# Differential attention in an encoder block: combining a tile's two score maps on GpSimd, undivided by the first map's sum, instead of on VectorE

## The chip, the cores and the metric

The kernel runs on one core of a Trainium2 chip, as one launch. The metric is device time in microseconds (us): median of three runs for the kernel before. The engines are TensorE (PE; its weight loads are listed as PEld), VectorE (DVE), ScalarE (ACT), GpSimd (POOL) and SyncE (SP), which issues the DMAs. Each works through its own list of instructions in order, and they wait for each other by semaphores.

## The reference

One encoder block for 1024 tokens of width 1024, with 16 meta tokens put in front (1040 keys), all in float32: an RMS norm, a projection, two attention branches, a gated merge, an output projection, then a SwiGLU feed-forward part and a last norm. The edit concerns branch A, differential attention with 4 heads, each with two score maps and one set of values of width 128:

```python
s1 = einsum('bqhd,bkhd->bhqk', q1, k1) * scale + bias
s2 = einsum('bqhd,bkhd->bhqk', q2, k2) * scale + bias
attn = softmax(s1, axis=-1) - lam * softmax(s2, axis=-1)
y = einsum('bhqk,bkhe->bqhe', attn, v)
...
y = rms_norm(y, subln_g) * (1.0 - lambda_init)   # y * rsqrt(mean(y*y) + EPS) * gain
```

Branch B is attention in a window; both branches are merged through sigmoid gates, which are projections of the block's input.

## The kernel before

The program is built by one long function, and a scheduler orders the instructions of ACT, DVE, POOL and SP by a simulated timeline. In branch A's attention PE is excepted: its order is the order in which the code issues its instructions, so it is written out by hand there.

**Stages.** First the input is normed and projected and branch B's attention is done (0 to some 330 us). Then follows branch A's attention, together with the projections of the gates (about 330 to 620 us). Then come the branches' output products, the merge, the output projection, and the feed-forward part by a scheme of seven products.

**Branch A's attention.** The work goes over 4 heads (h) and 8 tiles (t) of 128 queries, 32 tiles; "tile 3.2" is tile 2 of head 3. A string of slots, `SLOTS = "sgsgsngsgsgstntnt"` (in the last head `"sgsgsngsgsstntnt"`), says what PE is given for one tile after the other: `s` a step of this tile's scores, `g` a step of a gate projection (three matmuls of 512 columns, L199, which fill PE while other engines work), `t` a step of the transposes of the tile before (T_LAG = 1), `n` a step of the values or the norm of a pair of tiles before. All six `s` stand ahead of the first `t`. At the start of a head ten more gate steps stand in between, thirty at the first.

For one tile `scores_a` does the second map first (m = 1), then the first (m = 0). For each, PE makes the scores in three chunks of 352, 352 and 336 keys (L588, into banks of PSUM that rotate five deep under the tag "sc"; the transposes and the norm use the same banks). DVE subtracts the distance bias while it moves them to SBUF and keeps the running minimum (L594; the last chunk in two pieces, `no_dist` and `dist`). ACT takes the exponential of the 128x1040 map in place and sums its rows into `dn` (L599, followed by a read of the accumulator). DVE inverts the sum (L600). For m = 1 POOL scales the map by 1/sum and by -lambda (L602). For m = 0 DVE then makes the combined map, first map times 1/sum plus scaled second map (L605, one pass over 128x1040), and POOL copies 32 columns for the meta tokens (L606). The first map lies in one of two tiles `s0s`, the second in `s1` with two buffers.

One tile later `transpose_a` transposes the combined map on PE in groups of 4, 4 and 1 (L617, tile `apt`), ACT and DVE copy the result out as a high and a low part (L620, L621). `values_a` multiplies it with the values (L630) for pairs of tiles. `normed_a`, once for four tiles, squares the values (L637), sums the squares on PE (L643), forms mean plus EPS on DVE (L645), raises it to -1/2 on POOL (L646), and applies it (L651, L652).

Beside this, each of 16 gate columns needs its weights split into two parts: a copy on ACT (L111, `wh_c`) and a 128x1024 subtraction on POOL (L112, `wl_c`), and ACT copies the gate's results out (L539).

Of the kernel before, what the change touches and what calls it, by code (L numbers as in the profile page):

```python
# [9 lines left out]
F32 = mybir.dt.float32  # L10
F32R = mybir.dt.float32r
I32 = mybir.dt.int32
AF = mybir.ActivationFunctionType
ALU = mybir.AluOpType
# [4 lines left out]
P = 128  # L19
# [3 lines left out]
L = S + NM  # L23
# [8 lines left out]
EPS = 1e-6  # L32
# [2 lines left out]
SC = 5  # L35
N_WAIT = 3
PP2 = 2
COMBINE_POOL = (0, 1, 2, 3)
SLOTS = "sgsgsngsgsgstntnt"
SLOTS_LAST = "sgsgsngsgsstntnt"  # L40
S_BUFS = (2, 2)
# [28 lines left out]
def encoder_block(ctx: ExitStack, tc: tile.TileContext, x, meta, norm_mix, w_in, lq1, lk1, lq2, lk2,  # L70
                  subln, sink, w_ba, w_bb, w_o, norm_ffn, w_g, w_u, w_d, norm_final, out, dbg=None):
    nc = tc.nc
# [8 lines left out]
    def pool(name, side="left", space=None, bufs=1):  # L81
        kw = {} if space is None else {"space": space}
        if space is not DRAM:
            kw["reuse_waits"] = "tile"
        cm = tc.tile_pool(name=name, bufs=bufs, side=side, **kw)
        p = cm.__enter__()
        return p, lambda: cm.__exit__(None, None, None)
# [5 lines left out]
    def bank(p, tag, name, bufs):  # L93
        return p.tile([P, 512], F32, tag=tag, name=name, bufs=bufs)
# [267 lines left out]
    xts, xns, done, early = {}, {}, [], []  # L362
# [102 lines left out]
    neglam = acon.tile([P, 1], F32, name="neglam")  # L465
# [84 lines left out]
    apool, close_apool = pool("apool")  # L550
# [21 lines left out]
        nc.sync.dma_start(f32(v)[2 * NM:3 * NM, 0, 8, :], va_d[h][:NM, 1, 8, :])  # L572
        return qs, ks, v

    def scores_a(h, t, ld, s):
        slope = 2.0 ** -(2 * (h + 1))
        qs, ks, _ = ld
        nm = f"{h}_{t}"
        mn = small.tile([P, 2, 4], F32, tag="amn", name=f"amn_{nm}")
        dn = small.tile([P, 2], F32, tag="adn", name=f"adn_{nm}")  # L580
        u0 = 896 - t * P
        for m in (1, 0):
            s[m] = s0s[t % 2] if m == 0 else apool.tile([P, L], F32, tag="s1", name=f"as1_{nm}", bufs=S_BUFS[1])
            low = far_a
            for i, (k0, n) in enumerate(A_CHUNKS):
                ps = bank(psum2, "sc", f"aps_{nm}_{m}_{k0}", SC)
                for vv in range(2):
                    nc.tensor.matmul(ps[:, :n], qs[m][:, t * P:(t + 1) * P], ks[m][:, vv, k0:k0 + n],  # L588
                                     start=(vv == 0), stop=(vv == 1))
                parts = [(k0, min(k0 + n, S), dist[:, u0 + k0:u0 + min(k0 + n, S)])]  # L590
                if k0 + n > S:
                    parts.insert(0, (S, L, no_dist))
                for j, (a, b, far_by) in enumerate(parts):
                    nc.vector.tensor_tensor_reduce(s[m][:, a:b], ps[:, a - k0:b - k0], far_by, slope, low,  # L594
                                                   ALU.add, ALU.min, mn[:, m, i + j:i + j + 1])
                    low = mn[:, m, i + j:i + j + 1]
                if i < 2:
                    yield
            nc.scalar.activation(s[m][:, 0:L], s[m][:, 0:L], AF.Exp, bias=low, scale=-1.0, accum_out=dn[:, m:m + 1])  # L599
            nc.vector.reciprocal(dn[:, m:m + 1], dn[:, m:m + 1])  # L600
            if m:
                (nc.gpsimd if t % 4 in COMBINE_POOL else nc.vector).tensor_scalar(  # L602
                    s[1][:, 0:L], s[1][:, 0:L], dn[:, 1:2], neglam, ALU.mult, ALU.mult)
            yield
        nc.vector.scalar_tensor_tensor(s[0][:, 0:L], s[0][:, 0:L], dn[:, 0:1], s[1][:, 0:L], ALU.mult, ALU.add)  # L605
        nc.gpsimd.tensor_copy(s[0][:, L:L + 2 * NM].rearrange("p (a k) -> p a k", a=2),  # L606
                              s[0][:, S:L].unsqueeze(1).broadcast_to([P, 2, NM]))

    def transpose_a(h, t, s, at_):
        i = t % 2  # L610
        for b in range(3):
            nb = 4 if b < 2 else 1
            kp = P
            pt = bank(psum2, "sc", f"apt_{h}_{t}_{b}", SC).rearrange("p (k t) -> p k t", k=4)
            for j in range(nb):
                k = 4 * b + j
                nc.tensor.transpose(pt[:kp, j, :], s[:, k * P:k * P + kp], ident)  # L617
            hi = at_[:kp, 4 * b:4 * b + nb, 0, i * P:(i + 1) * P]
            lo = at_[:, 4 * b:4 * b + nb, 1, i * P:(i + 1) * P] if b < 2 else hi[:NM]
            nc.scalar.activation(hi, pt[:kp, :nb], AF.Copy)  # L620
            nc.vector.tensor_tensor(lo, pt[:lo.shape[0], :nb], f32(hi)[:lo.shape[0]], ALU.subtract)  # L621
            yield

    def values_a(h, t, v, at_, py):
        cols = slice(t % 4 // 2 * 256, t % 4 // 2 * 256 + 256)
        for part in range(3):
            for k in range(3 * part, 3 * part + 3):
                kp = P
                for j, (a, b) in enumerate(((0, 0), (0, 1), (1, 0)) if k < 8 else ((0, 0),)):
                    nc.tensor.matmul(py[:, cols], v[:kp, a, k, :], at_[:kp, k, b, :],  # L630
                                     start=(k == 0 and j == 0), stop=(k == 8))
            yield

    def normed_a(h, c, py):
        nm = f"{h}_{c}"
        ysq = apool.tile([P, 512], F32, tag="ysq", name=f"ysq_{nm}", bufs=1)
        nc.scalar.activation(ysq, py, AF.Square)  # L637
        yg = apool.tile([P, 512], F32, tag="yg", name=f"yg_{nm}", bufs=2)
        nc.scalar.activation(yg, py, AF.Copy, scale=gsub)
        yield  # L640
        pst = bank(psum2, "sc", f"apst_{nm}", SC)
        for i in range(4):
            nc.tensor.matmul(pst[:, i:i + 1], ysq[:, i * P:(i + 1) * P], ones, start=True, stop=True)  # L643
        f = small.tile([P, 4], F32, tag="af", name=f"af_{nm}", bufs=2)
        nc.vector.tensor_scalar(f, pst[:, 0:4], 1.0 / P, EPS, ALU.mult, ALU.add)  # L645
        nc.gpsimd.tensor_tensor(f, f, neg_half, ALU.pow)  # L646
        for _ in range(N_WAIT):
            yield
        pf = bank(psum2, "sc", f"apf_{nm}", SC)
        for i in range(4):  # L650
            nc.tensor.transpose(pf[:, i * P:(i + 1) * P], f[:, i:i + 1].broadcast_to([P, P]), ident)  # L651
        nc.vector.tensor_tensor(yg, yg, pf, ALU.mult)  # L652
        nc.sync.dma_start(ya_d[h][:, c * 512:c * 512 + 512], yg)
        yield
# [5 lines left out]
    def fill(n):  # L660
        while n > 0 and n_gates[0] > 0:
            n, n_gates[0] = n - 1, n_gates[0] - 1
            next(gates, None)


    acc = [None]

    def turn(done):
        h, t, s, at_, v = done
        yield from transpose_a(h, t, s[0], at_)  # L670

    def later(done):
        h, t, s, at_, v = done
        if t % 4 == 1:
            acc[0] = bank(psum2, "acc", f"apy_{h}_{t}", 1)
        yield from values_a(h, t, v, at_, acc[0])
        if t % 4 == 3:
            yield from normed_a(h, t // 4, acc[0])

    order_pe = tc.manual_schedule(engines={mybir.EngineType.PE})  # L680
    order_pe.__enter__()
    tiles, turning, tail = [], iter(()), []

    def step_tail():
        while tail and next(tail[0], True):
            tail.pop(0)

    for n in range(AH * NT + T_LAG):
        scoring, turning = iter(()), iter(())
        if n < AH * NT:  # L690
            h, t = divmod(n, NT)
            if t == 0:
                ld = load_a(h)
                fill(G_HEAD if h else G_FIRST)
            if t % 2 == 0:
                at_ = apool.tile([P, 9, 2, 256], F32R, tag="at", name=f"at{h}_{t}", bufs=AT_BUFS)
            s = [None, None]
            tiles.append((h, t, s, at_, ld[2]))
            scoring = scores_a(h, t, ld, s)
        if n >= T_LAG:  # L700
            turning = turn(tiles[n - T_LAG])
        for what in SLOTS if n < 3 * NT else SLOTS_LAST:
            if what == "s":
                next(scoring, None)
            elif what == "t":
                next(turning, None)
            elif what == "n":
                step_tail()
            else:
                fill(1)  # L710
        for _ in scoring:
            pass
        for _ in turning:
            pass
        if n >= T_LAG and tiles[n - T_LAG][1] % 2:
            tail.append(later(tiles[n - T_LAG]))
# [488 lines left out]
    for n in range(nf, len(steps)):  # L1205
# [4 lines left out]
        if p in LOADS:  # L1210
            at, half, col = LOADS[p]
            if at <= j < at + 4:
                t, cols = 4 * half + j - at, slice(col * 512, col * 512 + 512)
# [60 lines left out]
```

## Time and profile before

| | |
|---|---|
| device time, median of 3 runs | 1466.98 us (1464.96 to 1467.93) |
| the profiled execution | 1467.45 us |
| its span, first to last instruction | 1465.7 us (1.75 us lie around it) |
| mean granted clock of TensorE | 0.997 |
| busy in the span | PE 98%, DVE 59%, ACT 45%, POOL 36% |

A row of a table by stretch gives a stretch of the span, its length, then busy time of each engine (number of instructions), the granted clock of PE, the share of DMA. A row of groups gives line, engine, operation, output and inputs, shape, count, then busy us and mean ns, then idle us of the engine just ahead of it with what ended it. A timeline row gives start and duration in us, engine, line, operation, output<-inputs, and in brackets the idle time ahead of it and who ended it. A busy PE is not PE at its peak, since matmuls overlap. Names are cut: `as` is either map, `adn` its sums, `amn` the minima.

### The profile page before, as it was taken

The numbers are of one execution on the slowest core, as the hardware profiler recorded it, in microseconds if no ns is written. First come the engines' busy times: TensorE is split into PE (matmuls) and PEld (weight loads), VectorE is DVE, ScalarE is ACT, GpSimd is POOL, SyncE is SP. The second block draws the span as 40 slices with busy tenths as digits, with TensorE's granted clock in tenths as the row PEclk, the third lists the DMA queues.
The fourth block names the chain that finished last, engine by engine and source line by source line (L and its number), as shares of the span: only waits on it lengthen the run. The fifth ranks groups of instructions, "written<-read, shape, count | busy, mean of one in ns | idle before, by whom it ended". The sixth has DMA issues, their size and how long they took to land.

```text
span 1465.7 us, 21002 instructions
## 1 busy us (share of the span) xinstructions
PE 1439.6 (98%) x7353; PEld 1237.5 (84%) x7353; DVE 859.0 (59%) x1664; ACT 654.6 (45%) x1237; POOL 529.8 (36%) x502
## 2 busy tenths in 40 slices
PE   6999999999999999999999999999999999999998
PEld 6988989988898989877888878888888888888886
DVE  6356426528686868423613876555555554787667
ACT  5365436525455555445412744333333333444454
POOL 4143223313323232223822566454545442000444
PEclk9999999999999999999999999999999999999999
DMA  7334353272524251086531434333333323954443
GB/s 233 89 98 115 111 127 98 77 204 96 152 73 145 73 153 66 31 277 196 169 126 61 141 122 135 126 103 98 108 103 105 101 93 102 345 201 141 125 124 142
DMA packets 155577, 189.96 MB, mean 130 GB/s; under 512 B 16128, under 2 KB 101568, under 8 KB 155472
## 3 DMA queue, kind: packets, MB, share of 16 engines
q1 hardware_dynamic: 155472, 188.63, 40.9%
q8 instruction: 58, 0.95, 0.3%
q14 instruction: 47, 0.39, 0.1%
HBM read 128.09 MB, written 53.94 MB: 124 GB/s over the span
## 4 chain that ended last, share of the span: by engine, by line
PE 86%; POOL 4%; issue 4%; DMA 3%; ACT 1%; DVE 1%; SPq 1%; POOLq 0%; ACTq 0%; DVEq 0%
PE pg L1055 26%; PE pp_g L199 10%; PE pd L1149 8%; PE ppa L532 6%; PE po L832 6%; PE aps L588 4%; PE apy L630 3%; PE pp_va L199 3%; PE pp_qb L199 3%; PE pp_qa L199 3%; PE pp_ka L199 3%; POOL oa L112 3%; PE apt L617 2%; PE bpt L337 2%; PE bpy L343 2%
## 5 line engine op out<-in xcount | busy, mean ns | idle before, releaser
L1055 PE MATMUL pg<-t,wop 128*128 128x512 f32 x1056 | 242.9, 389 | 0.2 <-POOL wop L112 0.2
L1055 PEld LDWEIGHTS pg<-t,wop 128*128 128x128 f32 x1056 | 198.1, 188 | 41.7 <-POOL wop L112 0.6
L112 POOL TENSOR_TENSOR wop<-wf,wop 128x512 fp32r<-128x512 f32 x128 | 171.6, 1345 | 165.9 <-ACT wop L111 152.1
L1149 PE MATMUL pd<-ob,oa 128*128 128x512 f32 x924 | 210.2, 389 | 0.8 <-POOL oa L112 0.4
L1149 PEld LDWEIGHTS pd<-ob,oa 128*128 128x128 f32 x924 | 173.3, 188 | 37.6 <-POOL oa L112 0.8
L1055 PE MATMUL pg<-b,wop 128*128 128x512 f32 x792 | 184.0, 390 | 2.7 <-DVE c L1064 2.7
L1055 PEld LDWEIGHTS pg<-b,wop 128*128 128x128 f32 x792 | 148.3, 188 | 34.2 <-issue 2.4
L112 POOL TENSOR_TENSOR wl_c<-w_c,wh_c 128x1024 fp32r<-128x1024 f32 x31 | 74.9, 2418 | 155.2 <-ACT wh_c L111 144.8
L111 ACT ACTIVATE wop<-wf 128x512 fp32r<-128x512 f32 x128 | 80.2, 631 | 85.2 <-PE pg L1055 48.4
L599 ACT ACTIVATE as<-as,amn 128x1040 f32<-128x1040 f32 x64 | 74.5, 1165 | 72.7 <-DVE amn L594 72.7
L112 POOL TENSOR_TENSOR oa<-ra,oa 128x512 fp32r<-128x512 f32 x33 | 44.0, 1335 | 170.8 <-ACT oa L111 169.4
L199 PE MATMUL pp_g<-hT_hi,wh_c 128*128 128x512 f32 x256 | 101.4, 396 | 0.6 <-DMA g_d<-gate_stage 0.6
L199 PE MATMUL pp_g<-hT_hi,wl_c 128*128 128x512 f32 x256 | 100.9, 394 | 0.0
L199 PE MATMUL pp_g<-hT_lo,wh_c 128*128 128x512 f32 x256 | 100.9, 394 | 0.0
L111 ACT ACTIVATE oa<-ra 128x512 fp32r<-128x512 f32 x77 | 48.7, 632 | 107.7 <-PE pd L1149 50.2
L588 PE MATMUL aps<-ak,aq 128*128 128x352 f32 (+1 forms) x384 | 92.6, 326 | 0.0
L832 PE MATMUL po<-woh,mT 128*128 128x512 f32 x384 | 88.0, 390 | 0.0
L890 DVE TENSOR_TENSOR s<-wf,wf 128x512 f32<-128x512 f32 x22 | 26.8, 1217 | 103.9 <-DMA wf<-in_w_ff_gate_dram 56.2
L832 PEld LDWEIGHTS po<-woh,mT 128*128 128x128 f32 x384 | 71.9, 188 | 14.8
L588 PEld LDWEIGHTS aps<-ak,aq 128*128 128x128 f32 x384 | 69.6, 188 | 14.0
L594 DVE CUSTOM_DVE_ANT_0 as<-aps,dist,amn 128x352 f32<-128x352 f32 (+1 forms) x128 | 71.3, 564 | 10.4 <-PE aps L588 8.4
L324 POOL TENSOR_SCALAR bs<-bs,bdn 128x432 f32<-128x432 f32 (+1 forms) x64 | 37.0, 596 | 94.8 <-DVE bdn L322 81.4
(249 smaller groups left out, 2943.1 us busy)
## 6 DMA issues: line engine op xcount, KB each, us to landing
ra<-aop SPq DMA_DIRECT2D x77, 256.0 KB, 2.6
w_c<-in_w_in_dram SPq DMA_DIRECT2D x33, 512.0 KB, 4.0
wf<-in_w_ff_gate_dram SPq DMA_DIRECT2D x24, 512.0 KB, 3.8
wf<-in_w_ff_up_dram SPq DMA_DIRECT2D x24, 512.0 KB, 3.8
aop<-as SPq DMA_DIRECT2D x44, 256.0 KB, 2.1
aop<-c SPq DMA_DIRECT2D x33, 256.0 KB, 2.0
g_d<-gate_stage SPq DMA_DIRECT2D x32, 256.0 KB, 2.0
gt<-g_d SPq DMA_DIRECT2D x32, 256.0 KB, 3.4
```

The source lines that it names most:

```text
L111: nc.scalar.activation(hi, src, AF.Copy)
L112: lo_eng.tensor_tensor(lo, src, f32(hi), ALU.subtract)
L199: nc.tensor.matmul(ps[:, :n], a[:, c, :], b[:, c, at:at + n], start=(c == 0 and i == 0), stop=(c == DC - 1 and i == 2))
L324: nc.gpsimd.tensor_scalar(st[:, r, :W], st[:, r, :W], dn[:, r:r + 1], 1.0, ALU.mult, ALU.mult)
L532: nc.tensor.matmul(ps, w[:, a, j, :], src[j][:, b, tk], start=(j == 0 and n == 0), stop=(j == 3 and n == 2))
L588: nc.tensor.matmul(ps[:, :n], qs[m][:, t * P:(t + 1) * P], ks[m][:, vv, k0:k0 + n], start=(vv == 0), stop=(vv == 1))
L594: nc.vector.tensor_tensor_reduce(s[m][:, a:b], ps[:, a - k0:b - k0], far_by, slope, low, ALU.add, ALU.min, mn[:, m, i + j:i + j + 1])
L599: nc.scalar.activation(s[m][:, 0:L], s[m][:, 0:L], AF.Exp, bias=low, scale=-1.0, accum_out=dn[:, m:m + 1])
L630: nc.tensor.matmul(py[:, cols], v[:kp, a, k, :], at_[:kp, k, b, :], start=(k == 0 and j == 0), stop=(k == 8))
L832: nc.tensor.matmul(ps, mT[:, c, a, t * P:(t + 1) * P], wos[q, c][:, b], start=(c == 0 and n == 0), stop=(c == DC - 1 and n == 2))
L1055: nc.tensor.matmul(ps, op[:, x, c, :], b[:, y, c, :], start=(p in (1, 2, 5) and c == 0 and n == 0), stop=(p in (4, 2, 3) and c == 3 and n ...
L1149: nc.tensor.matmul(ps[u], oa[:, a, u * P:(u + 1) * P], ob[:, b, :], start=(p in (1, 2, 5) and j == 0 and k == 0), stop=(p in (2, 3, 4) and ...
```

## The change

The combined map is left undivided by the first map's sum d0. With d1 the second map's sum, the map is now e0 + c*e1 with c = -lambda*d0/d1, which is d0 times the map of before. The values come out d0 times as large, and so the norm's constant EPS becomes EPS*d0*d0 for that row, which gives the same normed values. The sums d0 are kept for four tiles in a tile `dns` with three buffers, since the norm needs them later.

DVE no longer makes the 128x1040 combination, nor inverts d0. It makes c (128x1). POOL scales the second map by c, which needs both sums and so both exponentials, and then adds it to the first.

```diff
-COMBINE_POOL = (0, 1, 2, 3)
...
-    def scores_a(h, t, ld, s):
+    def scores_a(h, t, ld, s, dns):
...
+        dn0, dn1, c = dns[:, t % 4:t % 4 + 1], dn[:, 0:1], dn[:, 1:2]
...
-            nc.scalar.activation(s[m][:, 0:L], s[m][:, 0:L], AF.Exp, bias=low, scale=-1.0, accum_out=dn[:, m:m + 1])
-            nc.vector.reciprocal(dn[:, m:m + 1], dn[:, m:m + 1])
+            nc.scalar.activation(s[m][:, 0:L], s[m][:, 0:L], AF.Exp, bias=low, scale=-1.0, accum_out=dn1 if m else dn0)
             if m:
-                (nc.gpsimd if t % 4 in COMBINE_POOL else nc.vector).tensor_scalar(
-                    s[1][:, 0:L], s[1][:, 0:L], dn[:, 1:2], neglam, ALU.mult, ALU.mult)
+                nc.vector.reciprocal(dn1, dn1)
             yield
-        nc.vector.scalar_tensor_tensor(s[0][:, 0:L], s[0][:, 0:L], dn[:, 0:1], s[1][:, 0:L], ALU.mult, ALU.add)
+
+        nc.vector.tensor_scalar(c, dn0, dn1, neglam, ALU.mult, ALU.mult)
+        nc.gpsimd.tensor_scalar(s[1][:, 0:L], s[1][:, 0:L], c, 1.0, ALU.mult, ALU.mult)
+        nc.gpsimd.tensor_tensor(s[0][:, 0:L], s[0][:, 0:L], s[1][:, 0:L], ALU.add)
...
-    def normed_a(h, c, py):
+    def normed_a(h, c, py, dn0):
...
-        nc.vector.tensor_scalar(f, pst[:, 0:4], 1.0 / P, EPS, ALU.mult, ALU.add)
+        nc.vector.scalar_tensor_tensor(dn0, dn0, EPS, dn0, ALU.mult, ALU.mult)
+        nc.vector.scalar_tensor_tensor(f, pst[:, 0:4], 1.0 / P, dn0, ALU.mult, ALU.add)
```

`turn` and `later` pass the new tile on, and one is made for every fourth tile. The new kernel's lines lie one lower up to the score loop (L111 becomes L110) and one or two higher behind it (L606 becomes L607, L617 L618, L621 L622, L646 L648). Its L604 is c, L605 the scaling, L606 the addition.

The scheduler orders ACT, DVE and POOL anew in this stage; the orders of PE and SP stay as they were. On POOL, around tile 1.2, the order was as follows (`as_1_2` is the second map of tile 1.2, `as_0` and `as_1` the two tiles for first maps, `wl_c` a weight split, `af` the power of a norm, `av` the next head's values):

```order
L602 TENSOR_SCALAR as_1_1_4360<-as_1_1_4360,adn_1_4359,neglam 128x1040
L569 MEMSET av_4223 128x128
L606 COPY as_1_3424<-as_1_3424 128x32
L602 TENSOR_SCALAR as_1_2_4459<-as_1_2_4459,adn_2_4458,neglam 128x1040
L646 TENSOR_TENSOR af_1_4522<-af_1_4522,neg_half 128x4
L112 TENSOR_TENSOR wl_c_4854<-w_c_4851,wh_c_4853 128x1024
L606 COPY as_0_3423<-as_0_3423 128x32
```

Now it is:

```order
L605 TENSOR_SCALAR as_1_1_4364<-as_1_1_4364,adn_1_4363 128x1040
L568 MEMSET av_4226 128x128
L606 TENSOR_TENSOR as_1_3424<-as_1_3424,as_1_1_4364 128x1040
L607 COPY as_1_3424<-as_1_3424 128x32
L648 TENSOR_TENSOR af_1_4524<-af_1_4524,neg_half 128x4
L605 TENSOR_SCALAR as_1_2_4463<-as_1_2_4463,adn_2_4462 128x1040
L111 TENSOR_TENSOR wl_c_4859<-w_c_4856,wh_c_4858 128x1024
L606 TENSOR_TENSOR as_0_3423<-as_0_3423,as_1_2_4463 128x1040
L607 COPY as_0_3423<-as_0_3423 128x32
```

The power now stands ahead of the tile's scaling, and the weight split between its scaling and its addition.

On ACT, around tile 3.2, the order was as follows (`wh_c` is the copy that the next split needs, `as_3_2` the second map of the tile, the next L599 its first map, `apt_1` the transposes of tile 3.1):

```order
L620 ACTIVATE at_0_5842<-apt_0_2_6014 128x128
L111 ACTIVATE wh_c_6461<-w_c_6459 128x1024
L539 COPY gate_stage<-pp_g_512_5935 128x512
L599 ACTIVATE as_3_2_6023,adn_2_6022<-as_3_2_6023,amn_2_6021 128x1040
L620 ACTIVATE at_0_5842<-apt_1_0_6074 128x4x128
L599 ACTIVATE as_0_3423,adn_2_6022<-as_0_3423,amn_2_6021 128x1040
```

Now it is:

```order
L621 ACTIVATE at_0_5853<-apt_0_2_6024 128x128
L599 ACTIVATE as_3_2_6035,adn_2_6034<-as_3_2_6035,amn_2_6033 128x1040
L110 ACTIVATE wh_c_6476<-w_c_6474 128x1024
L538 COPY gate_stage<-pp_g_512_5947 128x512
L621 ACTIVATE at_0_5853<-apt_1_0_6084 128x4x128
L599 ACTIVATE as_0_3423,dns_0_5854<-as_0_3423,amn_2_6033 128x1040
```

The tile's first exponential now stands ahead of the weight copy and of the gate's copy, which stood ahead of it. The same holds for tiles 0.6, 2.2 and 3.6. In the last tiles of a group of four (0.3, 0.7, 1.3, 2.3, 2.7, 3.3 and 3.7) ACT's second exponential also moved ahead of one or more of the copies of transposes (L620).

More of the change, by code (lines that the diff above doesn't have):

```diff
@@ L668, in turn @@
     def turn(done):
-        h, t, s, at_, v = done
+        h, t, s, at_, v, _ = done
         yield from transpose_a(h, t, s[0], at_)
     def later(done):
-        h, t, s, at_, v = done
+        h, t, s, at_, v, dn0 = done
         if t % 4 == 1:
@@ L677, in later @@
         if t % 4 == 3:
-            yield from normed_a(h, t // 4, acc[0])
+            yield from normed_a(h, t // 4, acc[0], dn0)
     order_pe = tc.manual_schedule(engines={mybir.EngineType.PE})
@@ L697, in encoder_block @@
             s = [None, None]
-            tiles.append((h, t, s, at_, ld[2]))
-            scoring = scores_a(h, t, ld, s)
+            if t % 4 == 0:
+                dn0 = apool.tile([P, 4], F32, tag="dns", name=f"dns_{h}_{t}", bufs=3)
+            tiles.append((h, t, s, at_, ld[2], dn0))
+            scoring = scores_a(h, t, ld, s, dn0)
         if n >= T_LAG:
```

## The prediction

> **What bounds the kernel now.** I read the page first, its row of busy times:
>
> ```profile
> PE 1439.6 (98%) x7353; PEld 1237.5 (84%) x7353; DVE 859.0 (59%) x1664; ACT 654.6 (45%) x1237; POOL 529.8 (36%) x502
> ```
>
> TensorE (PE) works 98% of the span, so only what stops or lengthens PE changes the time. The edited instructions all lie in branch A's attention; next comes the table by stretch for it, then the waits of PE in 330 to 610 us, then the groups by line:
>
> ```profile
> 334.00:606.00 272.00, 272.00 (x1672) 246.62 (x1670) 212.73 (x708) 147.00 (x273) 82.35 (x86) 1.00 0.31 99
> PE pp_g L199 <- DMA g_d<-gate_stage: 0.6, 1, 0.6
> L605 DVE SCALAR_TENSOR_TENSOR as<-as,adn,as 128x1040 f32<-128x1040 f32 x32 | 41.5, 1297 | 1.8 <-DVE adn L600 0.5
> L602 POOL TENSOR_SCALAR as<-as,adn,neglam 128x1040 f32<-128x1040 f32 x32 | 38.9, 1214 | 75.4 <-DVE adn L600 75.4
> L646 POOL TENSOR_TENSOR af<-af,neg_half 128x4 f32<-128x4 f32 x7 | 7.2, 1027 | 4.4 <-DVE af L645 4.4
> L112 POOL TENSOR_TENSOR wl_c<-w_c,wh_c 128x1024 fp32r<-128x1024 f32 x12 | 29.4, 2449 | 39.2 <-ACT wh_c L111 39.1
> ```
>
> The first row gives busy us of PE, PEld, DVE, ACT and POOL: in 272 us PE was busy for 272, VectorE (DVE) for 213, GpSimd (POOL) for 82. PE waits 0.6 us in the stage. So the 41.5 us that DVE is relieved of (L605) are worth at most that 0.6 us by themselves. What the edit can cost is a late operand for PE: PE's order is fixed, and the transposes L617 of a tile wait for the combined map. How early that map is now, in a usual tile (head 1, tile 4), shows in the timeline (start, duration):
>
> ```profile
> 434.24 0.16 DVE L600 RECIPROCAL adn<-adn 128x1 f32<-128x1 f32 x1
> 434.50 1.21 POOL L602 TENSOR_SCALAR as<-as,adn,neglam 128x1040 f32<-128x1040 f32 x1 [3.56 <-DVE adn L600]
> 437.37 0.16 DVE L600 RECIPROCAL adn<-adn 128x1 f32<-128x1 f32 x1
> 438.04 1.29 DVE L605 SCALAR_TENSOR_TENSOR as<-as,adn,as 128x1040 f32<-128x1040 f32 x1
> 442.77 0.49 PE L617 MATMUL apt<-ident,as 128*128 128x128 f32 x3
> ```
>
> The map is ready at 439.33 and its first transpose starts at 442.77: 3.44 us in hand.
>
> **The change, priced.** Per tile DVE loses a L605 (1.30 us) and the second reciprocal (0.16), and gains one 128x1 product, taken at the reciprocal's 0.16. POOL keeps its scaling pass (1.21), but behind the second exponential now, and gains a 128x1040 addition. That addition is not in the trace. The row of equal kind, the 128x1024 subtraction of L112, shows 2.45 us on average in this stage, 2.42 undisturbed; times 1040/1024 that is 2.46, my value. Its ends: not below the one-input pass of the same size, 1.21; not above 3.01, the longest such row:
>
> ```profile
> 421.26 0.16 DVE L600 RECIPROCAL adn<-adn 128x1 f32<-128x1 f32 x1
> 421.92 1.29 DVE L605 SCALAR_TENSOR_TENSOR as<-as,adn,as 128x1040 f32<-128x1040 f32 x1
> 419.62 1.21 POOL L602 TENSOR_SCALAR as<-as,adn,neglam 128x1040 f32<-128x1040 f32 x1 [5.21 <-DVE adn L600]
> 422.47 3.01 POOL L112 TENSOR_TENSOR wl_c<-w_c,wh_c 128x1024 fp32r<-128x1024 f32 x1 [0.64 <-ACT wh_c L111]
> 425.59 0.60 PE L617 MATMUL apt<-ident,as 128*128 128x128 f32 x4
> ```
>
> That split runs 0.6 us long, and a L605 of DVE was under way for its first 0.74 us. Every L605 leaves the stage, so I keep the undisturbed 2.46; at 3.01 the sum below would grow by 5 us (0.55 in each stop, and three more tiles stop). The Trainium skill ("SBUF — State Buffer", on the port pair that VectorE and GpSimd share) says that a VectorE instruction with two SBUF inputs and a GpSimd instruction that reads SBUF keep each other waiting. By that rule, too, the addition would take its undisturbed time, as the reductions of the stage read one operand from PSUM; the long row agrees with it.
>
> The chain after the second exponential is then: product 0.16, handover to POOL 0.10 (434.40 to 434.50 above), scaling 1.21, addition 2.46, handover to PE 0.15: **4.08 us**, counted from where the second reciprocal starts now. In the usual tile 437.37 + 4.08 = 441.45, before 442.77: no stall. I took the distance from second reciprocal to first transpose for all 32 tiles from the same view; the first and the last of them:
>
> ```profile
> 338.88 0.16 DVE L600 RECIPROCAL adn<-adn 128x1 f32<-128x1 f32 x1
> 341.01 0.33 PE L617 MATMUL apt<-ident,as 128*128 128x128 f32 x1
> 602.30 0.16 DVE L600 RECIPROCAL adn<-adn 128x1 f32<-128x1 f32 x1 [0.59 <-ACT as L599]
> 604.02 0.30 PE L617 MATMUL apt<-ident,as 128*128 128x128 f32 x1
> ```
>
> Distances are 2.13 and 1.72, so the shortages are 1.95 and 2.36. Of the others 23 are long enough (4.2 to 12.6). The short ones, as head.tile with the shortage: 0.1 1.41, 0.2 0.70, 0.4 0.13, 2.6 0.17, 3.2 1.51, 3.3 0.97, 3.6 1.50. Tile 1.2 (4.33) is long enough by itself, but POOL's new order puts a weight split of 2.42 between its scaling and its addition: 2.42 − 0.25 = 2.17.
>
> Shortages of neighbours don't add. PE has issued the scores of tile t+1 before it stops for tile t, so the stop also gives tile t+1's map time: its own stop is its shortage less the one before. 0.1 falls to 0, 3.3 to 0, 3.7 to 0.86. Sum: 1.95 + 0.70 + 0.13 + 2.17 + 0.17 + 1.51 + 1.50 + 0.86 = **9.0 us**.
>
> Two corrections. In tiles 0.6, 2.2, 3.2 and 3.6 the new order of ScalarE (ACT) puts the tile's first exponential ahead of a weight copy that feeds a POOL split, and POOL has that split and the power L646 ahead of the scaling. So far, in 3.2:
>
> ```profile
> 560.20 1.06 ACT L111 ACTIVATE wh_c<-w_c 128x1024 fp32r<-128x1024 f32 x1 [2.40 <-PE pp_g L199]
> 560.51 0.55 DVE L594 CUSTOM_DVE_ANT_0 as<-aps,dist,amn 128x320 f32<-128x320 f32 x1
> 561.63 1.16 ACT L599 ACTIVATE as<-as,amn 128x1040 f32<-128x1040 f32 x1
> 561.34 2.39 POOL L112 TENSOR_TENSOR wl_c<-w_c,wh_c 128x1024 fp32r<-128x1024 f32 x1 [3.38 <-ACT wh_c L111]
> 563.69 1.03 POOL L646 TENSOR_TENSOR af<-af,neg_half 128x4 f32<-128x4 f32 x1
> 564.32 0.19 ACT L599 ACTIVATION_READ_ACCUMULATOR as<-as,amn 128x1 f32 x1
> 564.91 0.16 DVE L600 RECIPROCAL adn<-adn 128x1 f32<-128x1 f32 x1
> 567.48 0.38 PE L617 MATMUL apt<-ident,as 128*128 128x128 f32 x2
> ```
>
> The first exponential needs a reduction that ends at 561.06. Without the 1.3 us of a L605 ahead of it that becomes about 559.75; the exponential with its read lasts 1.25, so the copy starts near 561.0 instead of 560.20, 0.8 us later. Copy, split and power follow (1.06, 2.39, 1.03, with 0.04 between), and scaling can start near 565.5; the chain above had it at 564.91 + 0.26 = 565.17. That is +0.3 each for 3.2 and 3.6. In 0.6 and 2.2 I take the slip as 0.9; their distance of 4.21 has 0.13 to spare, so about +0.75 each. Together +2.1. Against it, DVE no longer has L605 ahead of what the product waits for: in 3.2 the exponential's sum is read by 564.51 and the reciprocal starts 0.40 later. I take 0.4 off each of four stops (0.2, 3.2, 3.6, 3.7): −1.6. Sum 9.0 + 2.1 − 1.6 = **9.5 us**. The profiled execution took 1467.45, 0.47 above the median: 1467.45 + 9.5 = **1477**.
>
> Costed at nothing: eight 128x4 steps for the norm's constant (DVE, 0.16 each, long before use); the 128x32 copy behind the addition (0.21), covered by two groups of four transposes that need only the addition; the weight splits that slip by 1 to 4 us. A copy starts when PE lets go of the buffer, which is when it begins the column before, and that is every 26 us here:
>
> ```profile
> 421.33 1.06 ACT L111 ACTIVATE wh_c<-w_c 128x1024 fp32r<-128x1024 f32 x1
> 447.66 1.06 ACT L111 ACTIVATE wh_c<-w_c 128x1024 fp32r<-128x1024 f32 x1 [0.57 <-PE pp_g L199]
> ```
>
> So a split has some 20 us before PE needs it. Without such cover each step costs what it lasts or slips. Loads and stores keep their order, so no DMA moves. What comes late next is the release of PSUM banks: in most last tiles of a group of four ACT and DVE now serve the second exponential and the product ahead of the copies of the tile before's transposes, whose banks PE's next scores need. In 3.3 that release comes about 1.7 us after PE would want the bank, but PE has stopped 1.5 us in 3.2 by then; so I add nothing there.
>
> **Rivals.** *A. The stops above: 1473 to 1481.* *B. Relief eats most of the stops.* If DVE's backlog hides 1.3 us in each short tile, what remains is 0.0 (no L605 runs before it) with 1.95 and 1.2, whose split is fixed, with 2.17 less 0.4: 3.7 us, 1471. *C, not slower.* Same mechanism, further. In the last tile the reduction that the exponential waits for runs late behind L605 of the tile before:
>
> ```profile
> 596.92 0.32 PE L588 MATMUL aps<-ak,aq 128*128 128x352 f32 x1
> 600.37 0.54 DVE L594 CUSTOM_DVE_ANT_0 as<-aps,dist,amn 128x320 f32<-128x320 f32 x1
> ```
>
> Scores at 596.92, reduction at 600.37. If relief brings products forward by more than each shortage, from about 2.2 us on, PE never stops: 1467. Against it: a L605 is only 1.30, and nothing precedes tile 0.0. Gain is bounded by the 0.6 us wait. *D. Stops also slow PE's clock.* These are two idle stretches of PE and the table by stretch behind the first (PE busy, granted clock, DMA):
>
> ```profile
> 684.75 0.50 PE L532 MATMUL ppa<-ya,wbha 128*128 128x512 f32 x1 [1.66 <-ACT ya L111]
> 686.00:688.00 2.00, 1.74 (x6) 0.61 0.86 271
> 688.00:690.00 2.00, 2.00 (x5) 0.54 0.85 257
> 855.46 4.81 PE L1055 MATMUL pg<-b,wop 128*128 128x512 f32 x20 [1.99 <-DVE c L1064]
> 856.00:858.00 2.00, 2.00 (x10) 1.00 0.03 8
> ```
>
> After 1.66 us idle the clock fell to half for some 3.4 us (0.39 x 2 + 0.46 x 2 = 1.7 us lost); after 1.99 us it stayed full. So a stop of 1.5 to 2.2 us can cost 1.7 more. Four or five such stops make 7 to 8 us: 1485. The Trainium skill ("TensorE: Matmul & The Clock Gate", on the gate's two states) asks for an idle window of about 3.4 us; by it D would not occur, yet the first stretch shows that half of it can do.
>
> **How the numbers follow.** A 0.58, B 0.14, C 0.09, D 0.19. A is the likeliest, so its 1477 is the forecast. With the addition at 1.21 the same sum leaves 3.0 us of stops, or 3.5 with the corrections (1471); at 3.01 it makes 14.5 (1482), and with two of D's slow stretches 1485.5. The range is 1470 to 1486: it leaves out C (0.09) and the far end of D (some 0.06). About 0.2%, 2.9 us, is what a measurement tells from no change. C is within it, and a fifth of B: same 0.10. Faster gets 0.02, slower 0.88.
>
> **What would show it.** Each step right: L605 gone from DVE; a POOL addition near 2.46 us; PE idle before L618 (today's L617) with POOL as releaser, in nine to eleven tiles, 9 us in all, longest in 0.0, 1.2 and the last head; other stages unchanged. Wrong: no PE wait in the stage (C), PE waits on score banks instead, additions of 3 us, or granted clocks below 1 there (D).

## The result, and the profile after

| | before | after |
|---|---|---|
| median of 6 runs each | 1467.29 us (1464.96 to 1468.11) | 1476.60 us (1474.82 to 1480.02) |
| ratio, with its 95% interval | | 1.0069 (1.0058 to 1.0080) |
| the profiled execution: time, span, clock | 1467.45, 1465.7, 0.997 | 1475.66, 1473.9, 0.998 |

The change costs 9.3 us by the medians, and its profiled execution has a span 8.2 us longer. The page's row of busy times, the row of the stage (us of PE, PEld, DVE, ACT, POOL, then the granted clock) and the waits of PE from 330 to 625 us, in the new kernel:

```profile
PE 1440.5 (98%) x7353; PEld 1237.6 (84%) x7353; DVE 822.0 (56%) x1640; ACT 657.9 (45%) x1237; POOL 607.3 (41%) x534
```

```profile
334.00:606.00 272.00, 265.19 (x1615) 238.93 (x1613) 180.72 (x677) 145.78 (x266) 153.00 (x115) 1.00 0.31 98
```

```profile
PE apt L618 <- POOL as L606: 6.7, 5, 1.9
PE pp_g L198 <- ACT gate_stage L538: 1.0, 1, 1.0
```

DVE is relieved by 37 us over the whole span and that bought nothing. In the 272 us of the stage PE, which never stopped before, is now idle for 6.8, and the table of waits puts 6.7 of that down to one pair: the transposes L618 wait for POOL's addition L606. The granted clock stays at 1.00 there. The groups by line show what the new pieces of the chain take:

```profile
L604 DVE TENSOR_SCALAR adn<-dns,adn,neglam 128x1 f32<-128x1 f32 x32 | 8.7, 272 | 13.3 <-ACT as L599 13.3
L605 POOL TENSOR_SCALAR as<-as,adn 128x1040 f32<-128x1040 f32 x32 | 36.4, 1139 | 88.7 <-DVE adn L604 58.1 <-ACT at L621 14.4 <-PE aps L588 13.7
L606 POOL TENSOR_TENSOR as<-as,as 128x1040 f32<-128x1040 f32 x32 | 78.0, 2436 | 2.4
```

The stops themselves, from PE's timeline; the number in brackets is the idle time ahead of the transposes:

```profile
340.96 0.47 PE L588 MATMUL aps<-ak,aq 128*128 128x336 f32 x2
343.21 0.55 PE L618 MATMUL apt<-ident,as 128*128 128x128 f32 x3 [1.79 <-POOL as L606]
...
430.59 0.33 PE L618 MATMUL apt<-ident,as 128*128 128x128 f32 x1 [1.89 <-POOL as L606]
...
574.37 0.33 PE L618 MATMUL apt<-ident,as 128*128 128x128 f32 x1 [1.43 <-POOL as L606]
...
605.99 0.33 PE L618 MATMUL apt<-ident,as 128*128 128x128 f32 x1 [1.44 <-POOL as L606]
```

These are tiles 0.0, 1.2, 3.2 and 3.6; the fifth, 0.6, has 0.16. The idle time leaves out what PE takes to fill again. So I measure a stop by the distance from the start of the matmuls ahead to the start of the transposes, less the usual distance for that pair: for 0.0 that is 343.21 − 340.96 = 2.25, where 23 of the other tiles have 0.31, so 1.94. Counted this way the stage has stops of 8.1 us.

### The profile page after: what moved, and what is told of

Same layout as the page of the kernel before. It is cut to its first block, busy times and chain, and to the rows that moved or that the text cites. A ratio compares the mean times of both kernels' runs of the same rounds, so it can differ in the third digit from the quotient of the medians.

```text
span 1473.9 us, 21074 instructions
## 1 busy us (share of the span) xinstructions
PE 1440.5 (98%) x7353; PEld 1237.6 (84%) x7353; DVE 822.0 (56%) x1640; ACT 657.9 (45%) x1237; POOL 607.3 (41%) x534
## 4 chain that ended last, share of the span: by engine, by line
PE 82%; POOL 6%; DMA 4%; issue 4%; DVE 2%; ACT 1%; SPq 1%; POOLq 0%; ACTq 0%; DVEq 0%
PE pg L1059 27%; PE pp_g L198 9%; PE pd L1153 8%; PE po L836 6%; PE apy L631 3%; PE aps L588 3%; PE pp_va L198 3%; PE pp_qb L198 3%; PE pp_qa L198 3%; PE pp_ka L198 3%; PE ppa L531 3%; POOL oa L111 3%; PE apt L618 2%; PE bpt L336 2%; PE bpy L342 2%
## 5 line engine op out<-in xcount | busy, mean ns | idle before, releaser
L111 POOL TENSOR_TENSOR wop<-wf,wop 128x512 fp32r<-128x512 f32 x128 | 174.3, 1366 | 164.4 <-ACT wop L110 149.9
L111 POOL TENSOR_TENSOR wl_c<-w_c,wh_c 128x1024 fp32r<-128x1024 f32 x31 | 74.3, 2398 | 143.3 <-ACT wh_c L110 143.3
L110 ACT ACTIVATE wop<-wf 128x512 fp32r<-128x512 f32 x128 | 80.3, 632 | 84.6 <-PE pg L1059 51.8
L111 POOL TENSOR_TENSOR oa<-ra,oa 128x512 fp32r<-128x512 f32 x33 | 44.0, 1335 | 170.7 <-ACT oa L110 169.3
L599 ACT ACTIVATE as<-as,amn 128x1040 f32<-128x1040 f32 x64 | 74.6, 1165 | 76.4 <-DVE amn L594 64.3
L110 ACT ACTIVATE oa<-ra 128x512 fp32r<-128x512 f32 x77 | 48.7, 632 | 107.7 <-PE pd L1153 51.8
L606 POOL TENSOR_TENSOR as<-as,as 128x1040 f32<-128x1040 f32 x32 | 78.0, 2436 | 2.4
L894 DVE TENSOR_TENSOR s<-wf,wf 128x512 f32<-128x512 f32 x22 | 18.0, 818 | 108.7 <-DMA wf<-in_w_ff_up_dram 54.4
```

What stands on the lines that cost most here:

```text
L110: nc.scalar.activation(hi, src, AF.Copy)
L111: lo_eng.tensor_tensor(lo, src, f32(hi), ALU.subtract)
L606: nc.gpsimd.tensor_tensor(s[0][:, 0:L], s[0][:, 0:L], s[1][:, 0:L], ALU.add)
```

## The experiments

The theory: the cost is PE idle behind POOL's two passes. It is set tile by tile by the chain product, scaling, addition against PE's fixed order, and by what POOL has between or ahead of the two passes. The rivals: the undivided form itself costs something (product, norm constant), the weight splits on POOL alone are at fault, or the stops slow PE's clock. Each ratio is against runs of the kernel before in the same series, whose medians were 1467.61 for the first four experiments and 1468.38 for the others. Edits are against the changed kernel, if nothing else is said.

### One pass on VectorE

```diff
-        nc.gpsimd.tensor_scalar(s[1][:, 0:L], s[1][:, 0:L], c, 1.0, ALU.mult, ALU.mult)
-        nc.gpsimd.tensor_tensor(s[0][:, 0:L], s[0][:, 0:L], s[1][:, 0:L], ALU.add)
+        nc.vector.scalar_tensor_tensor(s[0][:, 0:L], s[1][:, 0:L], c, s[0][:, 0:L], ALU.mult, ALU.add)
```

> The undivided map is kept (c, the norm's constant), but the combination is one VectorE pass, first map plus c times second map, and both GpSimd passes are gone. Theory (PE stops because the map is ready late, behind two GpSimd passes of 1.14 and 2.44 us): product 0.27 plus one pass of about 1.30 is 2.0 us shorter than the changed kernel's chain, so no tile stops: 1467 us, within 1.5 of the kernel before. Rival (leaving the map undivided, its extra small steps or the new order of the queues cost the time): 1474 to 1477. A third view (VectorE's relief was worth something that the stops hide): above 1468.5, since the relief is given back here.

Measured: 1467.9 us, ratio 1.0000 (0.9991 to 1.0008). The waits of PE in the stage:

```profile
PE pp_g L198 <- ACT gate_stage L538: 2.1, 1, 2.1
PE aps L588 <- DMA ak<-ka_d: 0.2, 1, 0.2
```

No transpose waits. The algebra is free, and 32 scaling passes taken off POOL are worth nothing either. The cost of the change is the place of the combination.

### The two passes by halves

```diff
-        nc.gpsimd.tensor_scalar(s[1][:, 0:L], s[1][:, 0:L], c, 1.0, ALU.mult, ALU.mult)
-        nc.gpsimd.tensor_tensor(s[0][:, 0:L], s[0][:, 0:L], s[1][:, 0:L], ALU.add)
+        for at in (slice(0, 512), slice(512, L)):
+            nc.gpsimd.tensor_scalar(s[1][:, at], s[1][:, at], c, 1.0, ALU.mult, ALU.mult)
+            nc.gpsimd.tensor_tensor(s[0][:, at], s[0][:, at], s[1][:, at], ALU.add)
```

> The two GpSimd passes of the changed kernel are done by halves: scale and add columns 0 to 511, then 512 to 1039. The same work and two more instructions per tile, but the first group of four transposes can start some 1.6 us earlier. Theory (time from c to the first transpose decides): the stops of 1.4 to 1.9 us in tiles 0.0, 3.2 and 3.6 fall to 0 to 0.3, that of 1.2 stays if the weight split still stands ahead of an addition; 1468 to 1471. Rival (GpSimd's amount of work or the second half decides): 1476 or more.

Measured: 1473.95 us, ratio 1.0042 (1.0030 to 1.0055): a third of the cost gone, less than expected. POOL's and PE's rows around tile 1.2 (L606 is a scaling, L607 an addition here) show where the rest stays:

```profile
426.82 1.38 POOL L606 TENSOR_SCALAR as<-as,adn 128x512 f32<-128x512 f32 x2 [0.19 <-DVE adn L604]
428.17 1.30 POOL L607 TENSOR_TENSOR as<-as,as 128x512 f32<-128x512 f32 x1
429.42 2.39 POOL L111 TENSOR_TENSOR wl_c<-w_c,wh_c 128x1024 fp32r<-128x1024 f32 x1
430.67 0.60 PE L619 MATMUL apt<-ident,as 128*128 128x128 f32 x4
431.76 1.31 POOL L607 TENSOR_TENSOR as<-as,as 128x528 f32<-128x528 f32 x1
433.12 0.55 PE L619 MATMUL apt<-ident,as 128*128 128x128 f32 x3 [1.41 <-POOL as L607]
```

The first group of transposes is in time, but the weight split now stands between the two additions and stops the second group. In 0.0, 3.2 and 3.6 no split stands between the additions, and both groups are late: the first by 0.97, 0.63 and 0.63, and the second by 0.83, 0.44 and 0.44 more, since PE wants it less than 1 us behind the first. The scheduler put both scalings first, so that even the first half is ready only 2.65 us after its scaling begins; in 3.2 and 3.6 a split and the power also stand ahead of the scalings. Halving brings only the first group's half forward; what waits for the second half gains nothing.

### The gates' weight splits on VectorE

```diff
-            prepped[col] = prep(col, f"c{col}", lo_eng=nc.vector if col in (C_KB, C_QB) else None)
+            prepped[col] = prep(col, f"c{col}", lo_eng=nc.vector if col in (C_KB, C_QB) or col >= C_GA else None)
```

> The weight splits of the gate columns go to VectorE, the rest is the changed kernel. Theory: the splits that stand in GpSimd's queue ahead of the scaling (0.6, 2.2, 3.2, 3.6) or the addition (1.2) make their stops; without them 1.2 falls from 1.9 to 0, 3.2 and 3.6 from 1.4 to about 0.4, 0.0 stays at 1.8: about 3 us of stops, 1470 to 1472, unless VectorE's 12 new passes (1.1 to 2.4 us each) delay products. Rival (only the two passes of a tile count, the splits do not): 1475 to 1477.

Measured: 1478.23 us, ratio 1.0074 (1.0061 to 1.0087); missed on the high side. The stop in 1.2 fell to 0.81 and not to nothing; DVE's and POOL's rows there:

```profile
430.28 1.21 DVE L111 TENSOR_TENSOR wl_c<-w_c,wh_c 128x1024 fp32r<-128x1024 f32 x1
430.39 3.39 POOL L606 TENSOR_TENSOR as<-as,as 128x1040 f32<-128x1040 f32 x1
433.83 0.66 PE L618 MATMUL apt<-ident,as 128*128 128x128 f32 x4 [0.65 <-POOL as L606]
```

The addition starts 0.11 us into DVE's split and takes 3.39 us instead of 2.44. What is left of the split at that moment is 1.10; the addition is longer by 0.95. So it stood still beside it, and the experiment changed two things at once. 3.2 and 3.6 kept 1.24 and 1.25, since DVE, now with the split, made the product 0.63 later than the exponential's sum was read. The stops sum to 6.1 us only; the wait ahead of the stage was 3.1 in this profile (1.0 after the change), with some 1.7 lost to a lower clock behind it. Whether that wait comes with this kernel or with this execution isn't settled; but all five runs lie between 1477.3 and 1480.4 us, at mean clocks of 0.994 to 0.997, so something beyond the 6.1 comes with this kernel. So this run couldn't say what the splits cost; the next but one was made for that.

### The second map scaled twice

```diff
         nc.gpsimd.tensor_scalar(s[1][:, 0:L], s[1][:, 0:L], c, 1.0, ALU.mult, ALU.mult)
+        nc.gpsimd.tensor_scalar(s[1][:, 0:L], s[1][:, 0:L], 1.0, 1.0, ALU.mult, ALU.mult)
```

> The second map is scaled once more by 1.0 on GpSimd, which adds 1.14 us plus a gap of 0.08 to the chain of every tile. Theory: each tile stops longer by 1.22 less what it had to spare in the changed kernel's trace (0.06 to 2.97 us), less the stop that this adds in the tile before. Twelve tiles then add 0.6 to 1.2 each, 12.6 us in all: 1489, 1486 to 1492. If stops of neighbours add in full, 1.2 us more, which this run tells poorly. Rival (the queues' order, not the chain's length, makes the stops): 1476 to 1480.

Measured: 1500.18 us, ratio 1.0216 (1.0197 to 1.0235). The longest row of PE's waits and the stage's row:

```profile
PE apt L619 <- POOL as L607: 17.0, 10, 3.4
```

```profile
334.00:614.00 280.00, 262.21 (x1541) 235.00 (x1541) 171.37 (x635) 138.63 (x249) 172.21 (x136) 0.97 0.30 95
```

The direction is right: 1.2 us more on the chain stops PE in ten tiles. The size is missed by 11 us, mainly for two reasons. The scheduler put a weight split between second scaling and addition in tile 0.2 (a stop of 3.56), and with stops of about 3 us the stage's granted clock falls to 0.97, that is 0.03 x 280 = 8 us. So the rival of a slower clock is real for longer stops.

### The gates without a weight split

```diff
+        if col >= C_GA:
+            nc.scalar.activation(wh, w, AF.Copy)
+            return wh, wh
         wl = p.tile([P, DC, P], F32R, tag="wl", name=f"wl_{name}", bufs=bufs)
```

> The change as it is, but the 16 gate columns get no weight split: their low part is left out and the high part stands in its place in the products, so that PE has the same matmuls, and GpSimd loses the 128x1024 subtractions (2.4 us each), without giving them to any other engine. This leaves the gates' low part out of the result. Theory (what GpSimd has between or ahead of scaling and addition is part of the stops): the stop in tile 1.2 goes (2.04 to 0), as do those of 0.6 and 2.2 (0.3 each); 3.2 and 3.6 keep the chain's own shortage, 1.1 to 1.25 each, 0.0 its 1.95, 0.2 and 0.4 some 0.15 each. Stops 4.5 to 4.8 us, so 1472 us (1470.5 to 1473.5). Rival (the splits are not at fault, the chain alone is too long everywhere): stops as before, 1475 to 1477.

Measured: 1473.4 us, ratio 1.0031 (1.0021 to 1.0040), so +4.6. The stops in 0.6, 1.2 and 2.2 are gone; 0.0 has 2.4, 0.2 and 0.4 some 0.15 each. Tile 3.2 (L607 the product, L608 the scaling):

```profile
570.12 0.28 DVE L607 TENSOR_SCALAR adn<-dns,adn,neglam 128x1 f32<-128x1 f32 x1
570.49 1.15 POOL L608 TENSOR_SCALAR as<-as,adn 128x1040 f32<-128x1040 f32 x1 [0.81 <-DVE adn L607]
574.21 0.66 PE L621 MATMUL apt<-ident,as 128*128 128x128 f32 x4 [0.54 <-POOL as L609]
```

POOL now waits for the product instead of the other way round, and the stop is 0.70 by spacing (0.54 idle), where I had expected 1.1 to 1.25. The sum of the stops is 4.1. That 0.0 rose from 1.94 to 2.4 is not explained, and behind it this profile has a stretch of slow clock (0.57 in 346 to 348 us, 0.58 in 348 to 350). About half of the change's cost is thus POOL's other work standing in the way of the two passes, and about half is the chain's own length.

### PE's order with the transposes later

```diff
-SLOTS = "sgsgsngsgsgstntnt"
-SLOTS_LAST = "sgsgsngsgsstntnt"
+SLOTS = "sgsgsnsgsgsgtntnt"
+SLOTS_LAST = "sgsgsnsgssgtntnt"
```

> The change as it is, but in PE's hand-written order one gate step of each tile (0.7 us) is moved from between the fifth score step's neighbours to behind the last score step, so that the transposes come 0.7 us later after the scores. Theory: every stop loses 0.7: 0.0 1.94 to 1.2, 1.2 2.04 to 1.3, 3.2 and 3.6 1.6 to 0.9 each, the ones of 0.3 and less go; about 4.3 us of stops remain, 1472 us (1470.5 to 1473.5). Rival 1 (PE now waits for score banks instead, as VectorE gets the three chunks closer together): the gain is eaten, 1475 to 1477, with waits of the scores L588 on VectorE L594. Rival 2 (the distance does not decide): as the changed kernel, 1476.6.

The step that is moved stood ahead of the fourth score step. Measured: 1475.05 us, ratio 1.0047 (1.0033 to 1.0061); missed high. The stop in 0.0 fell from 1.94 to 0.76, and 1.2 has none, but 0.6 and 2.2 rose to 0.8 and 3.2 and 3.6 to 2.23. Tiles 1.2 and 3.2:

```profile
424.60 1.14 POOL L605 TENSOR_SCALAR as<-as,adn 128x1040 f32<-128x1040 f32 x1
425.82 2.43 POOL L606 TENSOR_TENSOR as<-as,as 128x1040 f32<-128x1040 f32 x1
428.21 2.40 POOL L111 TENSOR_TENSOR wl_c<-w_c,wh_c 128x1024 fp32r<-128x1024 f32 x1
429.10 0.60 PE L618 MATMUL apt<-ident,as 128*128 128x128 f32 x4
...
567.79 2.42 POOL L111 TENSOR_TENSOR wl_c<-w_c,wh_c 128x1024 fp32r<-128x1024 f32 x1
569.20 0.27 DVE L604 TENSOR_SCALAR adn<-dns,adn,neglam 128x1 f32<-128x1 f32 x1
570.18 1.15 POOL L605 TENSOR_SCALAR as<-as,adn 128x1040 f32<-128x1040 f32 x1
573.86 0.33 PE L618 MATMUL apt<-ident,as 128*128 128x128 f32 x1 [2.07 <-POOL as L606]
```

The scheduler answered the new slots by moving the splits. In 1.2 the split went behind the addition and its stop with it; in 3.2 the split, itself behind the power, stands ahead of the scaling until 570.18. There the product also starts only 2.43 us ahead of where the transposes would come (573.86 − 2.23 = 571.63, less 569.20), against 3.40 after the change alone. In the last head the second exponential follows the queues of ACT and DVE, and the slot moved behind the scores gave the transposes no time. Of the stop in 3.2, 1.66 is this distance (2.43 against a chain of 4.09) and 0.61 the split, which holds a scaling that could start at 569.57. Neither the theory's numbers nor the first rival held: PE doesn't wait for score banks, and the queues of ACT, DVE and POOL took the gain.

### The divided maps, combined on GpSimd

Against the kernel before:

```diff
-        nc.vector.scalar_tensor_tensor(s[0][:, 0:L], s[0][:, 0:L], dn[:, 0:1], s[1][:, 0:L], ALU.mult, ALU.add)
+        nc.gpsimd.tensor_scalar(s[0][:, 0:L], s[0][:, 0:L], dn[:, 0:1], 1.0, ALU.mult, ALU.mult)
+        nc.gpsimd.tensor_tensor(s[0][:, 0:L], s[0][:, 0:L], s[1][:, 0:L], ALU.add)
```

> The algebra of the kernel before (both maps divided, the norm's constant plain, no 128x4 squares), but the combination on GpSimd: the second map is scaled early as before, then the first map is scaled by the inverse of its sum and the two are added, both on GpSimd. The chain after the second exponential is the same as in the change, with the reciprocal (0.16) in place of the product (0.27); GpSimd has three passes a tile instead of two. Theory (the place of the combination costs, not the algebra): 1477 us (1475 to 1481), stops in the same tiles, 0.0 near 1.85, and some more where the third pass is in the way. Rival (the undivided form costs, through the product or the norm's constant): 1467 to 1469.

Measured: 1484.63 us, ratio 1.0108 (1.0095 to 1.0121); the direction as expected, 3.6 us above the upper end. The longest row of PE's waits, and then the stop of tile 1.2 and the row of the stretch behind it:

```profile
PE apt L618 <- POOL as L606: 9.8, 6, 2.2
```

```profile
432.82 0.44 PE L618 MATMUL apt<-ident,as 128*128 128x128 f32 x2 [1.88 <-POOL as L606]
```

```profile
434.00:436.00 2.00, 2.00 (x12) 2.00 (x10) 1.88 (x3) 0.77 (x2) 1.92 (x3) 0.51 0.29 103
```

The undivided form is not the cost: the form of before is stopped by the same pair of lines once it is on POOL. With a third pass per tile the stops lie in the same tiles, as expected, but several are longer: 1.07 and 1.05 in 0.6 and 2.2 (0.32 and 0.27 after the change), 2.38 and 2.37 in 3.2 and 3.6 (1.59 and 1.60). Half speed follows three of them: that in 1.2 (0.51 above), and those in 3.2 and 3.6 (0.50 in 582 to 584 and in 616 to 618 us). At 1.7 each that is 5 us, which accounts for the miss.

### Half on each engine

```diff
-        nc.gpsimd.tensor_scalar(s[1][:, 0:L], s[1][:, 0:L], c, 1.0, ALU.mult, ALU.mult)
-        nc.gpsimd.tensor_tensor(s[0][:, 0:L], s[0][:, 0:L], s[1][:, 0:L], ALU.add)
+        nc.gpsimd.tensor_scalar(s[1][:, 512:L], s[1][:, 512:L], c, 1.0, ALU.mult, ALU.mult)
+        nc.vector.scalar_tensor_tensor(s[0][:, 0:512], s[1][:, 0:512], c, s[0][:, 0:512], ALU.mult, ALU.add)
+        nc.gpsimd.tensor_tensor(s[0][:, 512:L], s[0][:, 512:L], s[1][:, 512:L], ALU.add)
```

> The undivided map, combined by halves on two engines: columns 0 to 511 by one VectorE pass, columns 512 to 1039 by GpSimd's scaling and addition. Theory: GpSimd's chain falls from 0.27+0.10+1.14+2.44 to about 0.27+0.10+0.6+1.25 = 2.2 us, 1.7 us less, and the second group of transposes that needs it starts 0.4 to 0.8 us behind the first; only tile 1.2 (if the weight split still stands ahead of the addition) can stop, by 0.5 to 1. Time 1467.5 to 1469. Rival (VectorE's pass with two SBUF inputs and GpSimd's passes hold each other up, as seen in a tile where the addition took 3.39 us): GpSimd's half takes 0.7 us longer, the addition or scaling shows means well above 0.6 and 1.25, and 1469 to 1472.

Measured: 1467.99 us, ratio 0.9996 (0.9987 to 1.0006). The one stop left in the table of waits is of 0.2 us. Two tiles (L605 the scaling, L607 the addition, L606 DVE's pass):

```profile
422.35 0.71 POOL L605 TENSOR_SCALAR as<-as,adn 128x528 f32<-128x528 f32 x1 [0.19 <-PE aps L588]
422.96 0.73 DVE L606 SCALAR_TENSOR_TENSOR as<-as,adn,as 128x512 f32<-128x512 f32 x1
423.14 1.74 POOL L607 TENSOR_TENSOR as<-as,as 128x528 f32<-128x528 f32 x1
...
429.06 0.75 DVE L606 SCALAR_TENSOR_TENSOR as<-as,adn,as 128x512 f32<-128x512 f32 x1
429.12 1.27 POOL L605 TENSOR_SCALAR as<-as,adn 128x528 f32<-128x528 f32 x1 [1.73 <-DVE adn L604]
430.48 1.32 POOL L607 TENSOR_TENSOR as<-as,as 128x528 f32<-128x528 f32 x1
```

Both held: the chain is short enough, and the engines do hold each other up. Scaling takes 0.71 by itself and 1.27 beside DVE's pass, the addition 1.32 and 1.74. The rival's mechanism is there, but a chain of some 3 us has room for it. No version beats the kernel before, as none can where PE had 0.6 us to win.

## Why the prediction was right, point by point

**The bound.** Right. The one pass on VectorE and the half on each show that DVE's and POOL's load are worth nothing; only PE's stops count.

**The chain.** 4.08 us was forecast. In tile 0.0 it is 343.21 − 339.18 = 4.03, from this product to the transposes shown above:

```profile
339.18 0.27 DVE L604 TENSOR_SCALAR adn<-dns,adn,neglam 128x1 f32<-128x1 f32 x1
```

In 0.2 and 0.4 it is 4.09. The terms are others: the product takes 0.27 and not the reciprocal's 0.16, the scaling 1.14 and not 1.21, the addition 2.44 where I took 2.46 (2.39 in tile 0.0), and the handover to PE 0.06 where I took 0.15, with 0.07 between the two passes. That these errors cancel is luck. The value chosen for the unseen addition, that of the subtraction of like size, was right, and its end of 3.01 was not a bad day but DVE at work beside it: without L605 no addition of the changed kernel is above 2.46. The Trainium skill ("SBUF — State Buffer", on the port pair that VectorE and GpSimd share) says that the one that comes second stands still until the first is done. The trace agrees where VectorE's instruction started first: 0.95 longer for 1.10 of overlap, and 0.56 for 0.69 (429.12 to 429.81). Where GpSimd's came first, it goes both ways. With the splits on VectorE, a split that began at 360.28 beside an addition of 359.20 to 361.64 took 2.45 and not 1.21; but with half on each engine, a scaling that began at 351.86 took 1.41, while VectorE's pass beside it, begun at 352.02, took its usual 0.74.

**The stops, tile by tile**, in us:

| tile | forecast | measured |
|---|---|---|
| 0.0 | 1.95 | 1.94 |
| 0.2, 0.4 | 0.3, 0.13 | 0.17, 0.15 |
| 0.6, 2.2 | 0.75 each | 0.32, 0.27 |
| 1.2 | 2.17 | 2.04 |
| 2.6, 3.7 | 0.17, 0.46 | none |
| 3.2, 3.6 | 1.4 each | 1.59, 1.60 |
| sum | 9.5 | 8.1 |

All the long stops are where they were forecast. That a stop gives the next tile time is shown by 3.7 alone, whose rows stand below: it would be some 0.57 short by itself, and doesn't stop. 0.1 and 3.3 don't stop either, as forecast, but not for the forecast's reason. From product to transposes they have 349.64 − 343.62 = 6.02 and 582.69 − 575.66 = 7.03; less the stops ahead of them, 1.94 and 1.59, that is 4.08 and 5.44, just enough and more than enough, where the kernel before had 2.67 and 3.11. In 1.2 the order of POOL did what its rows said:

```profile
424.69 1.14 POOL L605 TENSOR_SCALAR as<-as,adn 128x1040 f32<-128x1040 f32 x1 [0.19 <-PE aps L588]
425.80 2.40 POOL L111 TENSOR_TENSOR wl_c<-w_c,wh_c 128x1024 fp32r<-128x1024 f32 x1
428.15 2.38 POOL L606 TENSOR_TENSOR as<-as,as 128x1040 f32<-128x1040 f32 x1
```

**The two corrections** were each mis-sized. In 3.2 the sum was right by two errors against each other:

```profile
567.32 2.39 POOL L111 TENSOR_TENSOR wl_c<-w_c,wh_c 128x1024 fp32r<-128x1024 f32 x1 [1.47 <-ACT wh_c L110]
...
569.38 0.28 DVE L604 TENSOR_SCALAR adn<-dns,adn,neglam 128x1 f32<-128x1 f32 x1
569.68 1.01 POOL L648 TENSOR_TENSOR af<-af,neg_half 128x4 f32<-128x4 f32 x1
570.70 1.14 POOL L605 TENSOR_SCALAR as<-as,adn 128x1040 f32<-128x1040 f32 x1
```

With the product at 569.38 the scaling could start at 569.75; power and split hold it until 570.70. That is 0.95, where I had added 0.3. The relief of DVE was 0.83 (the distance from product to transposes is 572.78 − 569.38 = 3.40 without the stop, and was 2.57), where I had taken 0.4. The kernel without splits confirms the pair: the stop that is left, 0.70, is near 1.59 − 0.95 = 0.64. In 3.7 the relief was larger still. Its rows after the change:

```profile
607.27 0.27 DVE L604 TENSOR_SCALAR adn<-dns,adn,neglam 128x1 f32<-128x1 f32 x1 [1.39 <-ACT as L599]
...
612.39 0.60 PE L618 MATMUL apt<-ident,as 128*128 128x128 f32 x4
```

That is 5.12, less the 1.60 of the stop in 3.6: 3.52, where before it was 1.72. So in 3.7 the product comes 1.8 us earlier than before, and in 0.1 and 3.3 by 1.4 and 2.3: rival B's mechanism was right for these three tiles, and the 0.4 of the forecast too small. A L605 lasts only 1.30, so something else has a part in it, perhaps ACT's new order; the two were not separated. In 0.6 and 2.2 the slip of split and power was half of the 0.9 that I took:

```profile
384.37 0.27 DVE L604 TENSOR_SCALAR adn<-dns,adn,neglam 128x1 f32<-128x1 f32 x1
385.19 1.15 POOL L605 TENSOR_SCALAR as<-as,adn 128x1040 f32<-128x1040 f32 x1
```

With the product at 384.37 the scaling could start at 384.74, so it is 0.45 late.

**The sum.** Stops of 8.1 and a wait 0.4 longer ahead of the stage (1.0 against 0.6) make 8.5; the span grew by 8.2. The median grew by 9.3. Part of that difference can be the clock. The 0.4 need not come from the change: the wait ahead of the stage is between 0.6 and 3.1 us in the ten kept profiles. So the forecast of 1477 against 1476.6 is closer than its parts: the stops were forecast 1.4 too long, and about 1 us of the measured growth isn't stops. That these two nearly cancel is luck; the mechanism and the places of the long stops are not.

**Rival D.** The profiled execution of the changed kernel shows none of it in the stage. It has one slow stretch elsewhere (0.50 in 864 to 866 us), and so has that of the kernel before (the prediction's at 686), so their spans compare like with like. But the six runs fall apart by their mean granted clock, as span and clock of each show:

```
span 1473.9 clock 0.998    span 1474.8 clock 0.998    span 1476.0 clock 0.995
span 1473.0 clock 0.998    span 1474.8 clock 0.998    span 1478.2 clock 0.996
```

Two of six are 1 to 5 us longer at a lower clock. Where such a run was profiled, that of the kernel with PE's order changed (clock 0.995), one stretch stands right behind the stop of tile 3.2, and a second behind that of 3.6 (0.50 in 610 to 612 us). The first:

```profile
574.00:576.00 2.00, 2.00 (x13) 2.00 (x13) 0.98 (x4) 1.44 (x3) 0.72 (x2) 0.63 0.00 0
576.00:578.00 2.00, 2.00 (x12) 2.00 (x12) 1.36 (x3) 0.60 (x1) 1.92 (x2) 0.52 0.35 131
```

That costs 2 x 0.37 + 2 x 0.48 = 1.7 us, the price that the prediction gave one such stretch. In this stage of the ten kept profiles, all ten stops ahead of transposes with 2.06 us of idle time or more came with half speed, but only one (1.88) of the eight with 1.41 to 1.89. The changed kernel's four long stops have 1.43 to 1.89: that is why A and not D gave the time. Whether the two longer runs of the changed kernel had their stretches behind these stops was not seen, since they have no profile.

**What was costed at nothing** stayed so: the norm's constant, the copy of 32 columns and the release of the banks cause no wait of PE in the table of waits.

## What to carry to other kernels

Where one engine is busy all the time, its slack per operand, read tile by tile from the trace, is the price list: an edit that moves work off another engine can hardly gain, and it costs where the new chain is longer than that slack. Read the slack again after the edit, since the relieved engine's operands can come earlier (by 1.4 to 2.3 us in three tiles here). Read the new order of the engine that takes the work as well, since half of the cost here was other instructions that a scheduler put between or ahead of the two passes. And before work is moved from VectorE to GpSimd, see what else is on both at that moment: a pass with two operands took twice as long there, and more when both worked at once.

## What the runs showed of the hardware

- A 128x1024 subtraction took 1.21 us on VectorE and 2.40 on GpSimd, and GpSimd's additions cost little extra when cut: 1.30 and 1.31 by halves, 2.44 whole.
- A 128x1 product with two scalar operands took 0.27 us on VectorE, more than a reciprocal of the same shape (0.16).
- Half speed followed idle times of PE of 2.07 us (PE's order changed), 1.88 (divided maps on GpSimd) and 1.66 (before the change), but not those of 1.79 and 1.89 in the changed kernel, nor, behind the stage, those of 2.08 in the changed kernel (693.15) and of 2.63 without the weight splits (691.96). The Trainium skill ("TensorE: Matmul & The Clock Gate", on the gate's two states) has a free-running window of about 3.4 us, by which the moment of a stop would matter beside its length; that like stops go either way fits this. That a whole window must be idle does not fit the 1.66, the 1.88 and the 2.07. No run moved a stop alone in time, so what decides stays open.
